# Six edits to a two-layer decoder trunk: where the step sizes' projection stands, the order within a weight block, column tiles, row tiles, held blocks and the last norm

## The chip, the cores and the metric

The kernel runs on one core of one Trainium2 chip. The metric is the device time of one execution in microseconds (us). Three runs of the kernel before took 1283.12, 1284.42 and 1284.76; the median is 1284.42.

The names in the profile: PE is TensorE's matmuls, PEld its weight loads, DVE is VectorE, ACT is ScalarE, POOL is GpSimd, and SPq and POOLq are the queues on which SyncE and GpSimd issue DMAs.

## The reference

A residual stream `x` of 256 tokens by 2048 passes through two layers, each followed by `x = layer_norm(alpha * x + mixer(x))`, all in float32. Cut to what matters here:

```python
# layer 0: Mamba-2 SSD, 64 heads of 64 channels in 8 groups, state 128
z, xbc, dt = split(x @ w_in)                 # 4096 | 6144 | 64
xs, bm, cm = split(silu(conv4(xbc)))         # 4096 | 1024 | 1024
dt = softplus(dt + dt_bias)                  # the step sizes, 64 per token
y  = (cb * decay) @ (xs * dt) + d_skip * xs  # cb = cm @ bm.T, per head, causal
yg = rms_norm_per_group(y * silu(z)) * norm_g
h  = yg @ w_out                              # 4096 -> 2048
# layer 1: sparse attention, 32 heads of 128, latent of 256
c_q, c_kv, k_idx, w_idx, gate = split(x @ w_in)
s     = relu(q_idx @ k_idx.T)                # 16 index heads of 64
score = sum_over_heads(s * w_idx)            # causal; the best 64 keys stay
o     = softmax(masked(q_lat @ c_kv.T)) @ c_kv
h     = (uv(o) * silu(gate)) @ w_out         # 4096 -> 2048
```

## The kernel before

**Exact products from halves.** Weights arrive as blocks of 128 x 1024 (512 KB). ACT copies each to a rounded `hi` (L97) and DVE subtracts to get `lo` (L98). Activations are kept the same way, as a high and a low part side by side (`xT`, `yg`, `x1T`, `og`). A float32 product is then three rounded ones: hi by hi, hi by lo, lo by hi. Small products (`y`, `cb`, `ms`, `p_dt`, the scores, the attention) run in plain float32, which the profile shows as two matmuls for each one in the program.

**The stream.** The class `Stream` sets the order. Its units are the weight blocks in program order: 160 for layer 0's input projection, 64 for its output, 16 for layer 1's latents (three pairs of gate blocks behind them), 4 for the index queries, 32 for the heads mixed with the other gates (32 gates, two blocks each), and 64 for the last output projection. `run` first converts up to four blocks ahead (`SPLIT`), then issues a unit's matmuls, then one step of each active generator. `side(i, ...)` starts such a generator at unit `i`, so all small work is strewn between the units' matmuls in steps. `load` runs four blocks ahead of the conversion (`RAW`), on SPq. Both `hi` and `lo` have four buffers.

**A block of a column projection** (`stream_w`, with `mm3`): eight k-tiles of 128. For each a 512-wide matmul of `hi` with both parts of the activations, and then a 256-wide one of `lo` with the high part (L260, L261), into one PSUM tile `acc` (`g` for the gates).

**The start.** x comes in four quarters of 512 KB, with the weight blocks between them and `w_dt` behind. Units 0 and 1 run, then the 16 products of `p_dt` (L573), then the rest. `dt_steps` makes the step sizes from `p_dt`.

**A group of layer 0** is 20 units: B, C, four tiles of x, four of z. `m_steps` makes the decay products `M`, two heads to a step, `xst_steps` transposes x (`pxs`), and `y_steps(g, c)` multiplies them for one pair of heads: four products whose stationary side is 64 columns wide, written to PSUM partitions 0 to 63 or 64 to 127 (L391). DVE adds the skip and multiplies by the gate, ACT squares, and POOL adds the squares up over the four tiles. At the group's end a product with `sel` (1/512 in one column, 64 wide) sums them over the channels (`ms`, L412), and `norm_steps` runs for every second group.

**The scores** (`idx_steps`, L745 and L747): the keys of 64 channels lie twice in `kp`, once in the upper and once in the lower rows, with zeros in the other half, so that one product over 128 rows gives two index heads.

**The end** (`out_proj` and `last`): the last output projection makes four column blocks of 512 for two halves of 128 tokens. For the last one, the half-1 products of the last four weight blocks are held back, and follow the half-0 products, first their left 256 columns, then the right ones into the tile `part`. After that come the residual, the statistics, the inverse root in small steps (`rsqrt1_steps`), two steps over each of four 512-wide pieces (centre and gain; scale and offset), and the stores. The steps over some pieces run on ACT and POOL (`center_p`, `scale_p`), the others on DVE.

Of the kernel before, what the change touches and what calls it, by code (L numbers as in the profile page):

```python
# [16 lines left out]
P = 128  # L17
T = 256
# [34 lines left out]
HELD = 6  # L53
AHEAD = 2
# [69 lines left out]
def trunk_kernel(ctx: ExitStack, tc: tile.TileContext, x, xt, w1, wdt, dtp, prm, wo1,  # L124
# [46 lines left out]
    sel = cpool.tile([P, 2, 64], F32, tag="sel", name="sel")  # L171
# [85 lines left out]
    def mm3(ps, hk, lk, both, first, last):  # L257


        nc.tensor.matmul(ps, hk, both, start=first, stop=False, skip_group_check=True)  # L260
        nc.tensor.matmul(ps[:, 0:T], lk, both[:, 0:T], start=False, stop=last,  # L261
                         skip_group_check=True)
# [120 lines left out]
    def y_steps(g, c):  # L383
        ms = G[g].pop(("M", c))
        py = y_tile(f"y{g}_{c}")
        xsT = G[g][("xsT", c // 2)]
        for s in (0, 1):
            ws = slice(s * 256, 256 + s * 128)
            for k in (0, 1):
                ks = slice(64 * k, 64 * k + 64)  # L390
                nc.tensor.matmul(py[ks, s * P:T], xsT[:, s, c % 2, ks], ms[k][:, ws],  # L391
                                 start=(s == 0), stop=(s == 1), skip_group_check=True)
        yield
        vt = G[g][("x", c)]
        j = PC_SKIP + g * 4 + c
        v.scalar_tensor_tensor(vt, vt, par[:, j:j + 1], py[:, 0:T], op0=ALU.mult, op1=ALU.add)
        v.tensor_mul(vt, vt, G[g].pop(("z", c)))
        yield
        sq = sp2.tile([P, T], F32, tag="sq", name=f"sq{g}_{c}", bufs=3)
        nc.scalar.activation(sq, vt, AF.Square)  # L400
        yield
        if c:
            nc.gpsimd.tensor_add(sq, sq, G[g].pop("sq"))
        G[g]["sq"] = sq
        if c < 3:
            return
# [5 lines left out]
        nc.tensor.matmul(MS[b][0:64, 0:T], sel[:, k, :], sq, start=(k == 0), stop=(k == 1))  # L412
        yield
# [120 lines left out]
    for g in range(NG):  # L534
# [30 lines left out]
    split_x(0, 4)  # L565
    st.convert_to(1)
    split_x(4, 8)
    split_x(8, 12)
    st.convert_to(2)
    split_x(12, 16)  # L570
    st.run(DT_AT)
    for kt in range(KT):
        nc.tensor.matmul(p_dt[0:NH1, 0:T], w_dt[:, kt, :], xr[:, kt, :],  # L573
                         start=(kt == 0), stop=(kt == KT - 1))
    v.tensor_scalar_mul(convh, par[:, PC_CONV:PC_CONV + 240], 0.5)
# [113 lines left out]
    def kidx_steps(cell):  # L689
# [43 lines left out]
    def idx_steps(q, cell):  # L733
# [7 lines left out]
        for k in range(2):  # L741
            c = 2 * q + k
            pa = y_tile(f"sa{c}")
            pb = m_tile(f"sb{c}")
            nc.tensor.matmul(pa, qx[:, k, P:T], kp.rearrange("p a b -> p (a b)"),  # L745
                             start=True, stop=True)
            nc.tensor.matmul(pb[:, 0:T], qx[:, k, 0:P], kp[:, :, 0:P], start=True, stop=True)  # L747
# [453 lines left out]
```

## Time and profile before

| what | value |
|---|---|
| median of 3 runs | 1284.42 us |
| the profiled execution: its own time, its span | 1286.14 us, 1284.3 us |
| granted TensorE clock, mean | 0.991 |
| costliest on PE: `acc` L260, L261 | 458.3 us x1280, 360.3 us x1280 |
| `y` L391 on PE, 256 and 128 wide | 20.9 us x128, 12.4 us x128 |
| scores on PE: `sa` L745, `sb` L747 | 8.2 us x16, 4.8 us x16 |
| `ms` L412, `p_dt` L573 on PE | 5.2 us x16, 7.1 us x32 |
| splits: `hi` L97 on ACT, `lo` L98 on DVE | 423.7 us x404, 489.9 us x404 |
| first matmul, end of the last one | 7.23 us, 1265.87 us |

A row of the timeline has the start (us from the span's start), the duration, the engine, the line, the operation, out<-in with the shape, a count where equal rows are merged, and in brackets the idle time before it and what ended that. A row of a group has a count, then busy us and the mean ns of one, then idle time. A row of the waits has the sum, how many, the longest. Rows of PE overlap, since matmuls are pipelined; the end of one is modelled.

### The profile page before, as it was taken

The page shows a single profiled execution, that of the slowest core. Times are in us where ns is not written, and L with a number is a line of the kernel's source. Part 1 is how long each engine was busy: PE and PEld are TensorE (multiplying, and loading weights), DVE is VectorE, ACT ScalarE, POOL GpSimd, SP SyncE. Part 2 cuts the span into 40 slices and gives each one's busy share as a digit, 9 for nine tenths or more (in the row PEclk, how much of TensorE's full clock was granted, in tenths as well). Part 3 has the DMA queues.
Part 4 walks back from the last instruction along what each step waited for, and adds up shares of the span by engine and source line. Part 5 has one row for each costly group of instructions (what it writes and reads, how often), then busy time and mean ns, then how long its engine had stood idle before and what let it go on. Part 6 is the DMA issues. An engine that isn't in the chain of part 4 may idle for free.

```text
span 1284.3 us, 19045 instructions
## 1 busy us (share of the span) xinstructions
PE 1251.2 (97%) x7034; PEld 1069.6 (83%) x7034; DVE 915.9 (71%) x1680; ACT 702.0 (55%) x1194; POOL 83.8 (7%) x113
## 2 busy tenths in 40 slices
PE   7999999999999999999998999999999999999994
PEld 5888888888888888788886797999999998888883
DVE  5978787988798879756457577856666656566456
ACT  4556565656566666444335455566566666433332
POOL 1001111101110111110000000000000001000003
PEclk9999999999999999999999999999999999999997
DMA  7665566665656666676664463554444445866651
GB/s 254 207 193 181 181 182 194 178 205 175 204 176 195 182 198 179 179 249 203 197 191 156 164 220 129 181 164 148 158 155 149 148 154 166 336 208 189 195 179 66
DMA packets 65148, 236.51 MB, mean 184 GB/s; under 512 B 7896, under 2 KB 7904, under 8 KB 64672
## 3 DMA queue, kind: packets, MB, share of 16 engines
q1 hardware_dynamic: 60048, 215.12, 52.7%
q0 software_dynamic: 5008, 20.19, 4.6%
q8 instruction: 55, 0.90, 0.3%
q14 instruction: 37, 0.30, 0.1%
HBM read 231.00 MB, written 4.28 MB: 183 GB/s over the span
## 4 chain that ended last, share of the span: by engine, by line
PE 94%; DVE 3%; DMA 1%; ACT 1%; issue 0%; SPq 0%; DVEq 0%
PE acc L260 24%; PE acc L261 12%; PE g L260 9%; PE o L485 9%; PE o L486 8%; PE o L487 8%; PE g L261 5%; PE y L391 2%; PE q L814 1%; PE q L816 1%; PE q L815 1%; PE lg L832 1%; PE o L863 1%; PE pt L856 1%; PE pxs L373 1%; DMA scr<-in_xt_dram 1%
## 5 line engine op out<-in xcount | busy, mean ns | idle before, releaser
L98 DVE TENSOR_TENSOR lo<-raw,hi 128x1024 fp32r<-128x1024 f32 (+1 forms) x404 | 489.9, 1215 | 295.3 <-ACT hi L97 294.2
L97 ACT ACTIVATE hi<-raw 128x1024 fp32r<-128x1024 f32 (+1 forms) x404 | 423.7, 1051 | 314.9 <-PE o L487 171.8
L260 PE MATMUL acc<-xT,hi 128*128 128x512 f32 x1280 | 458.3, 402 | 8.1 <-DVE xT L553 8.1
L261 PE MATMUL acc<-xT,lo 128*128 128x256 f32 x1280 | 360.3, 282 | 0.4 <-DVE lo L98 0.4
L260 PEld LDWEIGHTS acc<-xT,hi 128*128 128x128 f32 x1280 | 241.6, 189 | 69.3 <-ACT hi L97 7.4
L261 PEld LDWEIGHTS acc<-xT,lo 128*128 128x128 f32 x1280 | 243.2, 190 | 0.9 <-DVE lo L98 0.9
L260 PE MATMUL g<-x1T,hi 128*128 128x512 f32 x512 | 188.2, 408 | 0.0
L261 PE MATMUL g<-x1T,lo 128*128 128x256 f32 x512 | 143.4, 280 | 0.0
L260 PEld LDWEIGHTS g<-x1T,hi 128*128 128x128 f32 x512 | 96.1, 188 | 21.2
L485 PE MATMUL o<-hi,yg 128*128 128x512 f32 x256 | 100.4, 392 | 0.0
L486 PE MATMUL o<-lo,yg 128*128 128x512 f32 x256 | 99.7, 390 | 0.0
L487 PE MATMUL o<-hi,yg 128*128 128x512 f32 x256 | 99.7, 389 | 0.0
L485 PE MATMUL o<-hi,og 128*128 128x512 f32 (+1 forms) x256 | 99.5, 389 | 0.0
L487 PE MATMUL o<-hi,og 128*128 128x512 f32 (+1 forms) x256 | 98.9, 386 | 0.0
L486 PE MATMUL o<-lo,og 128*128 128x512 f32 (+1 forms) x256 | 98.8, 386 | 0.0
L261 PEld LDWEIGHTS g<-x1T,lo 128*128 128x128 f32 x512 | 96.8, 189 | 0.5
L295 DVE SCALAR_TENSOR_TENSOR ca<-cr,convh,ca 128x255 f32<-128x255 f32 x144 | 69.3, 481 | 3.4
L485 PEld LDWEIGHTS o<-hi,yg 128*128 128x128 f32 x256 | 48.1, 188 | 10.9 <-issue 0.7
L487 PEld LDWEIGHTS o<-hi,yg 128*128 128x128 f32 x256 | 48.0, 188 | 10.1
L487 PEld LDWEIGHTS o<-hi,og 128*128 128x128 f32 x256 | 48.1, 188 | 9.9
L486 PEld LDWEIGHTS o<-lo,yg 128*128 128x128 f32 x256 | 48.1, 188 | 9.8
L485 PEld LDWEIGHTS o<-hi,og 128*128 128x128 f32 x256 | 48.1, 188 | 9.6
(246 smaller groups left out, 1688.5 us busy)
## 6 DMA issues: line engine op xcount, KB each, us to landing
raw<-in_w_dram SPq DMA_DIRECT2D x160, 512.0 KB, 3.9
raw<-in_wo_dram SPq DMA_DIRECT2D x128, 512.0 KB, 4.3
raw<-in_wg_dram SPq DMA_DIRECT2D x64, 512.0 KB, 3.3
raw<-in_wab_dram SPq DMA_DIRECT2D x32, 512.0 KB, 3.2
abc<-acs_d POOLq DMA_DIRECT2D x32, 256.0 KB, 4.1
raw<-in_wcq_dram SPq DMA_DIRECT2D x8, 512.0 KB, 4.4
raw<-in_wkv_dram SPq DMA_DIRECT2D x8, 336.0 KB, 6.3
scr<-in_xt_dram SPq DMA_DIRECT2D x4, 512.0 KB, 8.1
```

The source lines that it names most:

```text
L97: self.nc.scalar.activation(h[:, :w], r[:, :w], AF.Copy)
L98: eng.tensor_sub(l[:, :w], r[:, :w], h[:, :w].bitcast(F32))
L260: nc.tensor.matmul(ps, hk, both, start=first, stop=False, skip_group_check=True)
L261: nc.tensor.matmul(ps[:, 0:T], lk, both[:, 0:T], start=False, stop=last, skip_group_check=True)
L295: v.scalar_tensor_tensor(acc[:, d:], rw[:, :T - d], w(k), acc[:, d:], op0=ALU.mult, op1=ALU.add)
L373: nc.tensor.transpose(pm[:, o:o + P], G[g][("x", 2 * half + c)][:, s * P:(s + 1) * P], ident)
L391: nc.tensor.matmul(py[ks, s * P:T], xsT[:, s, c % 2, ks], ms[k][:, ws], start=(s == 0), stop=(s == 1), skip_group_check=True)
L485: nc.tensor.matmul(ps, ah, hs, start=(kk == 2 * first), stop=False)
L486: nc.tensor.matmul(ps, ah, ls, start=False, stop=False)
L487: nc.tensor.matmul(ps, al, hs, start=False, stop=(kk == 31))
L814: nc.tensor.matmul(ps, h[:, o:o + P], cqT[:, kt, 0:T], start=(kt == 0), stop=False)
L815: nc.tensor.matmul(ps, h[:, o:o + P], cqT[:, kt, T:2 * T], start=False, stop=False)
```

## The change

What it does, in six parts:
1. `w_dt` is the first transfer, x comes before the first weight block, and `p_dt`'s products stand before all units.
2. In `stream_w` the eight matmuls with `hi` come first, then the eight with `lo`; `mm3` is gone.
3. `y_steps` takes two pairs of heads at once, into two halves of one PSUM tile; it starts with the second pair's step. `sel` is 128 wide. The sum `ms` and the norm come one unit later.
4. The scores: `kp` holds the keys once in each half of the rows, without zeros. One index head's queries and keys lie in rows 0 to 63 and go to the tile `sa`, the other's in rows 64 to 127 and go to `sb`. ACT takes each tile in one 384-wide step.
5. Eight blocks are held at the end (`LAST`): the first four run 512 wide, the last four as before. The last four blocks get buffers of their own, in the room of the heads' pool, which is closed 24 units before the end.
6. The last norm runs on DVE alone. Each piece is stored after its scaling.

```diff
+LAST = 8
...
-    sel = cpool.tile([P, 2, 64], F32, tag="sel", name="sel")
+    sel = cpool.tile([P, 2, P], F32, tag="sel", name="sel")
...
             for k in range(8):
-                kt, ks = half * 8 + k, slice(k * P, (k + 1) * P)
-                mm3(cell["ps"], h[:, ks], l[:, ks], cell["x"][0][:, kt, :], kt == 0, kt == 15)
+                kt = half * 8 + k
+                nc.tensor.matmul(ps, h[:, k * P:(k + 1) * P], xs[:, kt, :], start=(kt == 0),
+                                 stop=False, skip_group_check=True)
+            for k in range(8):
+                kt = half * 8 + k
+                nc.tensor.matmul(ps[:, 0:T], l[:, k * P:(k + 1) * P], xs[:, kt, 0:T],
+                                 start=False, stop=(kt == 15), skip_group_check=True)
...
-    def y_steps(g, c):
-        ms = G[g].pop(("M", c))
+    def y_steps(g, half):
+        py = y_tile(f"y{g}_{half}")
+        xsT = G[g][("xsT", half)]
+        ms = [G[g].pop(("M", 2 * half + c)) for c in (0, 1)]
+        for c in (0, 1):
+            for s in (0, 1):
+                ws = slice(s * 256, 256 + s * 128)
+                for k in (0, 1):
+                    ks = slice(64 * k, 64 * k + 64)
+                    nc.tensor.matmul(py[ks, c * T + s * P:(c + 1) * T], xsT[:, s, c, ks],
+                                     ms[c][k][:, ws], start=(c == 0 and s == 0),
+                                     stop=(s == 1), skip_group_check=True)
...
-        nc.tensor.matmul(MS[b][0:64, 0:T], sel[:, k, :], sq, start=(k == 0), stop=(k == 1))
+        nc.tensor.matmul(MS[b][:, 0:T], sel[:, k, :], sq, start=(k == 0), stop=(k == 1))
...
-            st.side(u + 18 + max(gap * c, 2 * c), (y_steps, g, c))
+            if c % 2:
+                st.side(u + 18 + max(gap * c, 2 * c), (y_steps, g, c // 2))
...
-    load_x(0, 4)
-    st.load(0)
+    nc.sync.dma_start(w_dt, wdt)
+    load_x(0, 2)
+    load_x(2, 4)
     load_x(4, 8)
     load_x(8, 12)
-    st.load(1)
+    st.load(0)
     load_x(12, 16)
-    st.load(2)
-    nc.sync.dma_start(w_dt, wdt)
-    for i in range(3, RAW):
+    for i in range(1, RAW):
         st.load(i)
...
-            nc.tensor.matmul(pa, qx[:, k, P:T], kp.rearrange("p a b -> p (a b)"),
-                             start=True, stop=True)
-            nc.tensor.matmul(pb[:, 0:T], qx[:, k, 0:P], kp[:, :, 0:P], start=True, stop=True)
+            for a, w, b, n in ((P, T, 0, T), (0, P, T, P)):
+                for j in range(2):
+                    js = slice(64 * j, 64 * j + 64)
+                    nc.tensor.matmul(pj[j][:, b:b + n], qx[js, k, a:w], kp[js, 0:n],
+                                     start=True, stop=True, skip_group_check=True)
...
+        def normed2(half):
+            mv, rs, steps = mean(half)
+            for n in range(4):
+                next(steps, None)
+                next(steps, None)
+                center(half, n, mv)
+            now(steps)
+            for n in range(4):
+                scale(half, n, rs)
...
-        for a in held:
+        k = len(held) - 4
+        for a in held[:k]:
+            mm(*a, 1)
+        for a in held[k:]:
             mm(*a, 1, cols=(0, 256))
...
+    st.run(n_heads + 40)
+    heads.close()
+    wmore = ctx.enter_context(tc.tile_pool(name="wlast", bufs=4))
+    for i in range(len(st.units) - 4, len(st.units)):
+        st.homes[i] = wmore
```

Three places in the order of instructions. The first is PE at the end of group 1 of layer 0 and the beginning of group 2, before: the sum `ms`, the transposes `pxs` and the first `y` of group 2.

```order
L412 MATMUL ms_1398<-sq_3_1311,sel 64x256
L373 MATMUL pxs_1_1403<-ident,xs_2_1275 128x128 x2
L373 MATMUL pxs_1_1403<-ident,xs_3_1344 128x128 x2
L391 MATMUL y_0_1408<-M_1313,xsT_0_1240 64x256
L391 MATMUL y_0_1408<-M_1315,xsT_0_1240 64x256
L391 MATMUL y_0_1408<-M_1313,xsT_0_1240 64x128
L391 MATMUL y_0_1408<-M_1315,xsT_0_1240 64x128
L260 MATMUL acc_1381<-xT,hi_1321 128x512
```

The same place of the change, on PE: the transposes, one unit, the sum.

```order
L375 MATMUL pxs_1_1400<-ident,xs_2_1269 128x128 x2
L375 MATMUL pxs_1_1400<-ident,xs_3_1342 128x128 x2
L267 MATMUL acc_1380<-xT,hi_1319 128x512 x8
L271 MATMUL acc_1380<-xT,lo_1320 128x256 x8
L424 MATMUL ms_1433<-sq_3_1308,sel 128x256
```

And, four units further on, its first `y` of two pairs of heads.

```order
L395 MATMUL y_0_1551<-M_1311,xsT_0_1234 64x256
L395 MATMUL y_0_1551<-M_1313,xsT_0_1234 64x256
L395 MATMUL y_0_1551<-M_1311,xsT_0_1234 64x128
L395 MATMUL y_0_1551<-M_1313,xsT_0_1234 64x128
L395 MATMUL y_0_1551<-M_1466,xsT_0_1234 64x256
L395 MATMUL y_0_1551<-M_1468,xsT_0_1234 64x256
L395 MATMUL y_0_1551<-M_1466,xsT_0_1234 64x128
L395 MATMUL y_0_1551<-M_1468,xsT_0_1234 64x128
```

Before, `ms` and `y` stood with `pxs` in one stretch; now each of the three stands by itself, `ms` one unit later and `y` five, with twice the products.

The second place is the head of SP's queue, before (`scr` holds x and `w_dt`, `raw` the weight blocks):

```order
L549 DMA scr<-in_xt_dram 128x1024
L86 DMA raw_121<-in_w_dram 128x1024
L549 DMA scr<-in_xt_dram 128x1024 x2
L86 DMA raw_125<-in_w_dram 128x1024
L549 DMA scr<-in_xt_dram 128x1024
L86 DMA raw_128<-in_w_dram 128x1024
L562 DMA scr<-in_wdt_dram 128x1024
L86 DMA raw_131<-in_w_dram 128x1024
```

And SP's queue in the change:

```order
L568 DMA scr<-in_wdt_dram 128x1024
L562 DMA scr<-in_xt_dram 128x512 x2
L562 DMA scr<-in_xt_dram 128x1024 x2
L87 DMA raw_125<-in_w_dram 128x1024
L562 DMA scr<-in_xt_dram 128x1024
L87 DMA raw_128<-in_w_dram 128x1024
```

`w_dt` has moved from the eighth place to the first, and the first weight block from the second to behind three quarters of x.

The third place is DVE's last stretch, before: half 1 from its statistics (`t` and `rs` are the inverse root's steps, L1049 centres, L1053 scales).

```order
L1038 BN_AGGR mv_12509<-st_6175 128x2
L1039 TENSOR_SCALAR nm_12510<-mv_12509 128x1
L1040 TENSOR_SCALAR ve_12512<-mv_12509 128x1
L190 TENSOR_SCALAR t_12513<-ve_12512 128x1
L1049 SCALAR_TENSOR_TENSOR fin<-fin,mv_12509 128x512
L192 TENSOR_SCALAR rs_12511<-t_12513 128x1
L1049 SCALAR_TENSOR_TENSOR fin<-fin,mv_12509 128x512
L195 TENSOR_SCALAR t_12513<-rs_12511,ve_12512 128x1
L1053 SCALAR_TENSOR_TENSOR fin<-fin,rs_12480 128x512
L197 SCALAR_TENSOR_TENSOR rs_12511<-t_12513,rs_12511 128x1
L1053 SCALAR_TENSOR_TENSOR fin<-fin,rs_12480 128x512
```

And DVE's in the change, from the same step on:

```order
L1046 BN_AGGR mv_12511<-st_6160 128x2
L1047 TENSOR_SCALAR ve_12513<-mv_12511 128x1
L191 TENSOR_SCALAR t_12514<-ve_12513 128x1
L193 TENSOR_SCALAR rs_12512<-t_12514 128x1
L1056 SCALAR_TENSOR_TENSOR fin<-fin,mv_12511 128x512
L196 TENSOR_SCALAR t_12514<-rs_12512,ve_12513 128x1
L198 SCALAR_TENSOR_TENSOR rs_12512<-t_12514,rs_12512 128x1
L1056 SCALAR_TENSOR_TENSOR fin<-fin,mv_12511 128x512
```

Before, half 0's last scalings (with `rs_12480`) stood between half 1's steps, and some of half 1's centrings were on ACT and POOL; now all four of each half are DVE's, and half 0's stand ahead of half 1's.

More of the change, by code (lines that the diff above doesn't have):

```diff
@@ L255, in dt_steps @@
         yield
[L257 to L262, printed above, removed]
     def stream_w(half, cell, name):
@@ L381, in xst_steps @@
         yield
-    def y_steps(g, c):
-        ms = G[g].pop(("M", c))
[L385 to L392, printed above, removed]
-        yield
[L394 to L397, printed above, removed]
+    def y_steps(g, half):
[10 more added lines that the diff above has]
+                                     stop=(s == 1), skip_group_check=True)
+        yield
+        vts = [G[g][("x", 2 * half + c)] for c in (0, 1)]
+        for c, vt in enumerate(vts):
+            j = PC_SKIP + g * 4 + 2 * half + c
+            v.scalar_tensor_tensor(vt, vt, par[:, j:j + 1], py[:, c * T:(c + 1) * T],
+                                   op0=ALU.mult, op1=ALU.add)
+            v.tensor_mul(vt, vt, G[g].pop(("z", 2 * half + c)))
         yield
-        sq = sp2.tile([P, T], F32, tag="sq", name=f"sq{g}_{c}", bufs=3)
-        nc.scalar.activation(sq, vt, AF.Square)
+        sqs = [sp2.tile([P, T], F32, tag="sq", name=f"sq{g}_{2 * half + c}", bufs=3)
+               for c in (0, 1)]
+        for vt, sq in zip(vts, sqs):
+            nc.scalar.activation(sq, vt, AF.Square)
         yield
-        if c:
+        if half == 0:
+            nc.gpsimd.tensor_add(sqs[1], sqs[1], sqs[0])
+            G[g]["sq"] = sqs[1]
+            return
+        for sq in sqs:
             nc.gpsimd.tensor_add(sq, sq, G[g].pop("sq"))
-        G[g]["sq"] = sq
-        if c < 3:
-            return
+            G[g]["sq"] = sq
+        yield
         yield
@@ L700, in kidx_steps @@
         yield
-        for k in range(2):
-            ks = slice(64 * k, 64 * k + 64)
-            v.tensor_copy(A["kp"][ks, k, :], pm[ks, 0:T])
+        v.tensor_copy(A["kp"], pm[:, 0:T])
         yield
@@ L1071, in last @@
+        for a in held[k:]:
             mm(*a, 1, cols=(0, 256))
-        for a in held:
-            mm(*a, 1, part=part[:, 0:256], cols=(256, 512), first=held[0][1])
+        for a in held[k:]:
+            mm(*a, 1, part=part[:, 0:256], cols=(256, 512), first=held[k][1])
         c3 = r[:, 1, 1536:2048]
         now(residual2(3, 0, cell))
-        mv, nm, rs, steps = mean(0)
-        for n in (0, 1, 3):
-            center_p(0, n, nm)
-        next(steps)
-        center(0, 2, mv)
-        for _ in range(3):
-            next(steps)
+        normed2(0)
@@ L1084, in last @@
         v.scalar_tensor_tensor(c3, c3, ALPHA, cell["ps"][1], op0=ALU.mult, op1=ALU.add)
-        next(steps)
         v.bn_stats(sts[:, 1, 6, :], c3[:, 0:256])
-        now(steps)
-        scale_p(0, 0, rs)
-        scale_p(0, 1, rs)
-        rs0 = rs
         v.tensor_add(c3[:, 256:512], c3[:, 256:512], part[:, 0:256])
         v.bn_stats(sts[:, 1, 7, :], c3[:, 256:512])
-        mv, nm, rs, steps = mean(1)
-        center_p(1, 0, nm)
-        center_p(1, 1, nm)
-        for n in (2, 3):
-            next(steps)
-            center(1, n, mv)
@@ L1099, in last @@
-        for n in (2, 3):
-            next(steps)
-            scale(0, n, rs0)
-        for n in (0, 1, 2, 3):
-            store(0, n)
-        now(steps)
-        scale_p(1, 0, rs)
-        for n in (2, 1, 3):
-            scale(1, n, rs)
-        for n in (2, 1, 0, 3):
-            store(1, n)
+        normed2(1)
     L["tail2"] = last
```

61 lines of the change are left out of this document (24 added, 37 removed).

## The prediction

> **What bounds the kernel now.** I read the page from its top, then TensorE's waits, then the timeline of single places: a run of the stream, the start, a switch, the end.
>
> ```profile
> PE 1251.2 (97%) x7034; PEld 1069.6 (83%) x7034; DVE 915.9 (71%) x1680; ACT 702.0 (55%) x1194; POOL 83.8 (7%) x113
> PE 94%; DVE 3%; DMA 1%; ACT 1%; issue 0%; SPq 0%; DVEq 0%
> PE acc L260 <- DVE xT L553: 8.1, 2, 7.2
> ```
>
> TensorE is busy 97% of the span and is 94% of the chain that ended last; its largest wait is the 8.1 us at the start. So between the first and the last matmul nearly nothing but fewer or shorter steps on TensorE saves time. Matmuls overlap, so a row's duration is not its price: the price is the distance from its start to the next start, and I use such distances. The rest of the time lies at the two ends, before TensorE starts and after its last matmul.
>
> **First all high parts of a block, then all low ones.** Rows: first and last of 21 pairs in a row, of 11 pairs, of 66 matmuls 512 wide, of six such, and of 23 that are 256 wide; then the weight loads and the split on DVE.
>
> ```profile
> 112.94 0.40 PE L260 MATMUL acc<-xT,hi 128*128 128x512 f32 x1
> 120.36 0.40 PE L260 MATMUL acc<-xT,hi 128*128 128x512 f32 x1
> 123.85 0.39 PE L260 MATMUL acc<-xT,hi 128*128 128x512 f32 x1
> 127.66 0.39 PE L260 MATMUL acc<-xT,hi 128*128 128x512 f32 x1
> 1240.23 0.39 PE L485 MATMUL o<-hi,og 128*128 128x512 f32 x1
> 1255.19 0.39 PE L485 MATMUL o<-hi,og 128*128 128x512 f32 x1
> 698.27 0.39 PE L612 MATMUL qp<-hi,x1T 128*128 128x512 f32 x1
> 699.66 0.39 PE L612 MATMUL qp<-hi,x1T 128*128 128x512 f32 x1
> 1262.83 0.28 PE L485 MATMUL part<-hi,og 128*128 128x256 f32 x1
> 1265.59 0.28 PE L487 MATMUL part<-hi,og 128*128 128x256 f32 x1
> L261 PEld LDWEIGHTS acc<-xT,lo 128*128 128x128 f32 x1280 | 243.2, 190 | 0.9 <-DVE lo L98 0.9
> L98 DVE TENSOR_TENSOR lo<-raw,hi 128x1024 fp32r<-128x1024 f32 (+1 forms) x404 | 489.9, 1215 | 295.3 <-ACT hi L97 294.2
> ```
>
> A pair costs 0.353 in the long run (7.42 / 21) and 0.346 in the other (3.81 / 11); between them 0.351, nearer to the longer. Alone, 512-wide matmuls cost 0.227 (`o`) or 0.232 (`qp`), 256-wide ones 0.120. A block of eight pairs is 2.81 us now; grouped it would be 8 x 0.227 + 8 x 0.120 = 2.78, or 2.82 with 0.232. There are 224 such blocks (160 and 64). The ends are -11 us (0.227 throughout, and 0.117 for the low ones) and +2; I take **-5.0 us**, from 0.227, which the longer of the two rows has, and low ones between 0.117 and 0.120. That the low parts are needed later saves nothing: TensorE hardly waits for them (0.9 us in the row of the loads).
>
> The Trainium skill ("TensorE: Matmul & The Clock Gate", Part 3, The mechanism, on what overlaps and what doesn't) says that a weight load overlaps matmuls in flight only when its row group differs. By that rule the eight low matmuls would each pay their load; the trace disagrees so far, with 0.120 between starts.
>
> **The step sizes' projection first.** ACT's first rows start when a transfer of 512 KB has landed: the first, the fifth and the sixth of the queue. Then come a 512-wide matmul of that time, and `p_dt` with what follows it.
>
> ```profile
> 4.76 1.06 ACT L552 ACTIVATE xT<-scr 128x1024 fp32r<-128x1024 f32 x1 [2.68 <-DMA scr<-in_xt_dram]
> 11.99 1.06 ACT L97 ACTIVATE hi<-raw 128x1024 fp32r<-128x1024 f32 x1 [0.23 <-DMA raw<-in_w_dram]
> 13.47 1.06 ACT L552 ACTIVATE xT<-scr 128x1024 fp32r<-128x1024 f32 x1 [0.41 <-DMA scr<-in_xt_dram]
> 12.60 0.63 PE L260 MATMUL acc<-xT,hi 128*128 128x512 f32 x1
> 17.82 7.12 PE L573 MATMUL p_dt<-scr 128*64 128x256 f32 x32
> 24.87 0.50 PE L260 MATMUL acc<-xT,hi 128*128 128x512 f32 x1
> ```
>
> The 16 products of `p_dt` take 7.05 us, 0.44 each, where TensorE has other work. In the changed queue `w_dt` is first, x's quarters are transfers 2, 3, 4 and 6 (the first of them cut in two), and the first weight block is transfer 5. So `p_dt` can start at about 5.4 (4.76 and half a transfer), and its last four products wait for transfer 6: they end at 13.47 + 4 x 0.44 = 15.2 at the earliest. But TensorE is slow at first: 0.63 us at 12.60 where the runs above have 0.39. With products at double price until about 13 us they end near 16.2. Block 0 landed at 11.99 and is split by 14.3; its 8 pairs and the next 8 take 5.6. The third block starts at 21.8, not 24.87: **-3.1 us**. Bounds: -4.1 (end at 15.2) and +0.8 (double price for all 16, about 14 us from 5.4 and a gap, an end at 20).
>
> **Heads' outputs by four, ones 128 wide.** The first four rows show one `y` between two pairs, the next two the sum of squares `ms`. Then come the scores, which use the whole array.
>
> ```profile
> 104.81 0.28 PE L261 MATMUL acc<-xT,lo 128*128 128x256 f32 x1
> 105.02 0.87 PE L391 MATMUL y<-M,xsT 128*64 128x256 f32 x8
> 105.82 0.50 PE L260 MATMUL acc<-xT,hi 128*128 128x512 f32 x1
> 106.15 0.28 PE L261 MATMUL acc<-xT,lo 128*128 128x256 f32 x1
> 136.07 0.65 PE L412 MATMUL ms<-sq,sel 128*64 128x256 f32 x2
> 136.65 0.66 PE L373 MATMUL pxs<-ident,xs 128*128 128x128 f32 x4
> ...
> 771.57 0.28 PE L730 MATMUL ix<-cqT,lo 128*128 128x256 f32 x1
> 771.69 1.02 PE L745 MATMUL sa<-sC 128*128 128x512 f32 x2
> 772.55 0.59 PE L747 MATMUL sb<-sC 128*128 128x256 f32 x2
> 772.80 0.47 PE L728 MATMUL ix<-cqT,hi 128*128 128x256 f32 x1
> 773.11 0.28 PE L729 MATMUL ix<-cqT,hi 128*128 128x256 f32 x1
> ```
>
> A 512-wide float32 product costs 0.86 us (`sa` to `sb`), 1.68 ns a column. From 771.57 to 773.11 are 1.54 us: 1.29 of products and 0.24 of the two 256-wide matmuls beside them. Entry and exit cost 0.01 while the whole array is used. In `y`, two products on 64 columns run side by side, so its 384 columns should take 0.65. From 104.81 to 106.15 are 1.34, less 0.35 for one pair: 0.99. Switching to half the columns and back costs **0.34 us**. `ms` is 64 wide too and shows the exit: 0.58 for 256 columns, not 0.43. There are 32 switches for `y` and 8 for `ms`; 16 stay. 24 x 0.34 = **-8.2 us**. Bounds: -5.4 if `ms` gains nothing, and -8.6. The steps of DVE, ACT and POOL for `y` stay the same in number and lie beside TensorE's stream.
>
> One wait is new: in the last group the third `M` needs a buffer that the first `y` of four still reads, so DVE stands until that `y` is done. Behind it stand one more `M`, one `xsT`, two `E` and the next `lo`, none longer than `lo`'s 1.2 us; I estimate 4. TensorE has two blocks split ahead, 24 matmuls of 0.227, 5.4 us: 0, at worst 1.
>
> **Scores on row halves.** Eight times 1.29 now, half of it products with zeros. If the halves run side by side as `y`'s do, they take 8 x 0.65 = 5.2, and the five places where they stand switch to half the rows: 5 x 0.34 = 1.7. So 10.3 becomes 6.9: **-3.4 us**. No row shows two row halves. Bounds: -5.1 (the switch is free) and +1.7 (one after the other). I take side by side, from `y`, the nearest row. The Trainium skill ("TensorE: Matmul & The Clock Gate", Part 3, The mechanism) says that tiles on different row groups overlap; no run here shows it.
>
> **The end.** DVE's rows, then the stores.
>
> ```profile
> 1262.39 0.74 DVE L1049 SCALAR_TENSOR_TENSOR fin<-fin,mv 128x512 f32<-128x512 f32 x1
> 1266.78 0.41 DVE L1091 TENSOR_TENSOR fin<-fin,part 128x256 f32<-128x256 f32 x1
> 1268.34 0.15 DVE L190 TENSOR_SCALAR t<-ve 128x1 int32<-128x1 int32 x1
> 1269.56 1.68 DVE L1049 SCALAR_TENSOR_TENSOR fin<-fin,mv 128x512 f32<-128x512 f32 x1
> 1274.63 0.26 DVE L195 TENSOR_SCALAR t<-rs,ve 128x1 f32<-128x1 f32 x1
> 1275.12 0.27 DVE L195 TENSOR_SCALAR t<-rs,ve 128x1 f32<-128x1 f32 x1
> 1275.62 3.08 DVE L1053 SCALAR_TENSOR_TENSOR fin<-fin,rs 128x512 f32<-128x512 f32 x3
> out_dram<-fin SPq DMA_DIRECT2D x8, 256.0 KB, 2.0
> ```
>
> TensorE ends at 1265.59 + 0.28 = 1265.9, DVE at 1278.7: 12.8 us. DVE is late because half 0 is not finished when TensorE is, and because the same step that takes 0.74 takes 1.68 beside POOL's work. With eight blocks held, half 1 takes 24 x 0.227 + 48 x 0.120 = 11.2 us behind half 0, and half 0's chain (statistics, then the steps below, some 9 us) ends before that. After TensorE's end remain: the sum and the statistics, 1.6 (1266.78 to 1268.34); eight steps at about 0.70, 5.6; the inverse root, three rounds of 0.49, in part hidden between them, and its start, 1.4. Together 8.6: **-4.2 us**. The last store lands 2.0 us behind 1278.7, and the span ends 3.5 us after that, at 1284.3, with no row there. POOL has no work left at the end, which may shorten this by 0 to 3: I take **-1.5**. Term: **-5.7**, bounds -3 and -7.5. For this, the held blocks must be split at one per six matmuls, 1.36 us; DVE's 1.2 fits, with little to spare.
>
> **Sum.** -5.0 - 3.1 - 8.2 - 3.4 - 5.7 = **-25.4 us**. The profiled execution took 1286.1 (its span and 1.8 around it), 1.7 over the median of 1284.4. So 1260.7 for such an execution, and 1259.0 as a median.
>
> **Rivals.**
> - The row halves run one after the other (against: `y`; for: no row): five us less gain, 1284.4 - 20.3 = 1264.1.
> - The grouped stream gains nothing or loses up to 2 (for: `qp` at 0.232): 1264 to 1266.
> - Start and end give nothing, because the slow clock stretches `p_dt` and DVE meets another wait: 1267.8.
> - Slower: the eight low loads in a row are not hidden. If the low matmuls came at the load's 0.190 instead of 0.117, that is 1792 x 0.073 = +131, and with the other four terms (-20.4) 1395. It decides from 11 ns per low matmul, 0.128 between starts. Against it: 0.120 in 23 gaps, each with a load of its own. The rule quoted above would give this.
>
> **Chances.** Forecast 0.60; row halves 0.13; grouping 0.16; start and end 0.05; exposed loads 0.04; nothing of it shows 0.02. Within 0.2% a measurement of this kernel can't tell a difference from none. Faster 0.94, same 0.02, slower 0.04. The range takes the good ends of grouping and tail together below, and lost row halves with lost grouping above: 1249 to 1272.
>
> **What would show it.** `p_dt` done before 17 us and the third block before 23; 16 `y`, each about 1.6 us between its neighbours, and `ms` as cheap as the scores' entry; `sa` and `sb` starting within 0.02 us of each other; eight 512-wide starts at 0.227 to 0.232, then eight near 0.12; DVE's last step some 8.6 us behind TensorE's last matmul. Wrong if the low starts lie at 0.13 or more, if `sa` and `sb` start 0.2 apart, or if TensorE shows new waits for `hi` or `lo`.

## The result, and the profile after

Four runs of the changed kernel took 1260.48 to 1262.22 us, median **1261.53**; before, four runs took 1283.12 to 1284.76, median 1284.41. The ratio is **0.9823, 95% interval 0.9810 to 0.9837**: faster by 1.8%, 2.5 us short of the forecast median of 1259.0 and inside the predicted range. The profiled execution took 1262.22, its span is 1260.5; before, the span was 1284.3. Two executions among the experiments took far longer (3182.70 us in u10_y_early, 2524.32 in u12_group_alone) and are in no ratio below; without them the medians of these two are 1259.99 and 1282.00.

The page of the changed kernel, its first part and the shares of the chain that ended last, and then TensorE's waits (us in total, times, longest):

```profile
PE 1235.4 (98%) x7066; PEld 1072.6 (85%) x7066; DVE 909.4 (72%) x1685; ACT 692.3 (55%) x1186; POOL 68.6 (5%) x104
PE 93%; DVE 4%; DMA 1%; issue 1%; ACT 0%; SPq 0%; DVEq 0%; ACTq 0%
```

```profile
PE p_dt L578 <- DMA scr<-in_xt_dram: 6.0, 3, 5.3
PE o L497 <- DVE zs L278: 0.8, 1, 0.8
PE cb L324 <- DVE C L306: 0.3, 1, 0.3
PE pxs L375 <- DVE xs L306: 0.3, 1, 0.3
```

TensorE is still what bounds the kernel. The wait at the start is 2 us shorter, and three small waits are new, all for VectorE; the largest is that of the first output projection for `zs`.

Where the time went can be read stretch by stretch. The table is worked out from the starts of the matmuls in the two traces. "Blocks" is the sum of the distances from one matmul of the stream to the next; "small work" is the sum of the distances from a block's last matmul to the next block's first, where anything stands between them (what it delays behind that first matmul counts as blocks). The prediction's -5.0 for grouping is spread over the 224 blocks.

| stretch (us) | before | after | measured | predicted |
|---|---|---|---|---|
| to the third block | 24.87 | 20.82 | -4.05 | -3.1 |
| third block to first `qp`: blocks | 443.4 | 440.7 | -2.7 | -3.5 |
| the same stretch: small work (`y`, `ms`, `pxs`, `cb`) | 47.7 | 40.4 | -7.35 | -8.2 |
| the same stretch: the first output projection | 180.1 | 180.6 | +0.5 | 0 |
| first `qp` to the first head (with the scores) | 116.8 | 113.3 | -3.6 | -3.8 |
| heads, gates, last output projection | 452.8 | 452.9 | +0.1 | -1.1 |
| last matmul's end to the span's end | 18.4 | 11.7 | -6.7 | -5.7 |
| sum | | | -23.8 | -25.4 |

The rows of the changed kernel's timeline that answer to those shown before: the start; one `y` of four heads between two blocks; one `ms`; the first scores.

```profile
5.32 3.62 PE L578 MATMUL p_dt<-scr 128*64 128x256 f32 x8 [5.32 <-DMA scr<-in_xt_dram]
9.41 3.67 PE L578 MATMUL p_dt<-scr 128*64 128x256 f32 x16 [0.47 <-DMA scr<-in_xt_dram]
13.25 1.94 PE L578 MATMUL p_dt<-scr 128*64 128x256 f32 x8 [0.17 <-DMA scr<-in_xt_dram]
15.12 2.11 PE L267 MATMUL acc<-xT,hi 128*128 128x512 f32 x8
...
20.82 2.00 PE L267 MATMUL acc<-xT,hi 128*128 128x512 f32 x8
...
83.78 1.11 PE L271 MATMUL acc<-xT,lo 128*128 128x256 f32 x8
84.82 1.52 PE L395 MATMUL y<-M,xsT 128*64 128x256 f32 x16
86.27 2.14 PE L267 MATMUL acc<-xT,hi 128*128 128x512 f32 x8
...
133.27 1.11 PE L271 MATMUL acc<-xT,lo 128*128 128x256 f32 x8
134.22 0.59 PE L424 MATMUL ms<-sq,sel 128*128 128x256 f32 x2
134.46 2.20 PE L267 MATMUL acc<-xT,hi 128*128 128x512 f32 x8
...
757.96 0.48 PE L756 MATMUL sa<-sC 64*128 64x256 f32 x1
757.97 0.48 PE L756 MATMUL sb<-sC 64*128 64x256 f32 x1
758.28 0.38 PE L756 MATMUL sa<-sC 64*128 64x256 f32 x1
758.29 0.38 PE L756 MATMUL sb<-sC 64*128 64x256 f32 x1
```

The first eight matmuls of `p_dt` take 3.62 us and the next sixteen 3.67: TensorE is at half speed only for the first ones. `y` of four heads takes 1.45 (84.82 to 86.27) where two `y` before took 2 x 0.80; `ms` takes 0.24 where it took 0.58. `sa` and `sb` start 0.01 apart, and the next two 0.32 later, again together: the row halves do run side by side.

The end: TensorE's last matmul, VectorE's last steps, the stores (start of the first issue, and time to the end of the last one; the stores take 2.1 us to land).

```profile
1248.51 0.28 PE L499 MATMUL part<-hi,og 128*128 128x256 f32 x1
1248.83 0.42 DVE L1088 TENSOR_TENSOR fin<-fin,part 128x256 f32<-128x256 f32 x1 [1.20 <-PE part L499]
1254.38 2.73 DVE L1060 SCALAR_TENSOR_TENSOR fin<-fin,rs 128x512 f32<-128x512 f32 x4
1244.61 12.87 SPq L1062 DMA_DIRECT2D out_dram<-fin  x8
```

VectorE now waits for TensorE (1.20 us) before it closes half 1: half 0 was done in time. It ends at 1257.1, 8.3 us behind TensorE (12.8 before), and the span ends 3.4 us after that (5.6 before).

### The profile page after: what moved, and what is told of

Its sections match the earlier page's. It is cut to its first block, busy times and chain, and to the rows that moved or that the text cites. A ratio compares the mean times of both kernels' runs of the same rounds, so it can differ in the third digit from the quotient of the medians.

```text
span 1260.5 us, 19096 instructions
## 1 busy us (share of the span) xinstructions
PE 1235.4 (98%) x7066; PEld 1072.6 (85%) x7066; DVE 909.4 (72%) x1685; ACT 692.3 (55%) x1186; POOL 68.6 (5%) x104
## 4 chain that ended last, share of the span: by engine, by line
PE 93%; DVE 4%; DMA 1%; issue 1%; ACT 0%; SPq 0%; DVEq 0%; ACTq 0%
PE acc L267 22%; PE acc L271 11%; PE g L267 9%; PE o L497 9%; PE o L499 9%; PE o L498 9%; PE g L271 5%; PE y L395 2%; DVE lo L99 1%; PE q L822 1%; PE q L823 1%; PE q L824 1%; PE lg L840 1%; PE o L871 1%; PE pt L864 1%; DMA scr<-in_xt_dram 1%
## 5 line engine op out<-in xcount | busy, mean ns | idle before, releaser
L267 PE MATMUL acc<-xT,hi 128*128 128x512 f32 x1280 | 324.7, 395 | 0.0
L267 PEld LDWEIGHTS acc<-xT,hi 128*128 128x128 f32 x1280 | 230.3, 189 | 43.0 <-ACT E L350 0.9
L271 PEld LDWEIGHTS acc<-xT,lo 128*128 128x128 f32 x1280 | 174.5, 190 | 12.8
L271 PE MATMUL acc<-xT,lo 128*128 128x256 f32 x1280 | 178.3, 282 | 0.0
L267 PE MATMUL g<-x1T,hi 128*128 128x512 f32 x512 | 134.2, 404 | 0.0
L267 PEld LDWEIGHTS g<-x1T,hi 128*128 128x128 f32 x512 | 92.8, 188 | 17.9
L271 PEld LDWEIGHTS g<-x1T,lo 128*128 128x128 f32 x512 | 69.8, 190 | 5.1
L271 PE MATMUL g<-x1T,lo 128*128 128x256 f32 x512 | 71.3, 282 | 0.0
L300 ACT ACTIVATE cr<-ca 128x256 f32<-128x256 f32 x48 | 20.1, 418 | 88.1 <-DVE ca L297 88.1
L499 PEld LDWEIGHTS o<-hi,og 128*128 128x128 f32 x256 | 48.1, 188 | 9.9
```

Of the source, the lines that this page charges most:

```text
L267: nc.tensor.matmul(ps, h[:, k * P:(k + 1) * P], xs[:, kt, :], start=(kt == 0), stop=False, skip_group_check=True)
L271: nc.tensor.matmul(ps[:, 0:T], l[:, k * P:(k + 1) * P], xs[:, kt, 0:T], start=False, stop=(kt == 15), skip_group_check=True)
L300: nc.scalar.activation(rw, acc, AF.Tanh)
L499: nc.tensor.matmul(ps, al, hs, start=False, stop=(kk == 31))
```

## The experiments

Twelve kernels, each timed in five rounds against the kernel before, whose medians in the three series were 1283.44, 1283.49 and 1283.58. Since these differ a little from the 1284.41 beside the changed kernel, the last column compares ratios: the variant's less 0.9823, times 1284. Each ratio has an interval of about +-0.0013, 1.7 us, so a difference in that column under some 2.4 us is not sure by the times alone; there the stretches of the trace have to carry the reading. A drop of the granted clock that lasts 3.4 us in some traces and 6.8 in others makes about 1 us of difference between them (last section).

| variant | median us | ratio, 95% interval | against the changed kernel, us |
|---|---|---|---|
| u1_pairs | 1260.02 | 0.9815 (0.9802 to 0.9829) | -1.0 |
| u8_mirror | 1261.02 | 0.9824 (0.9810 to 0.9837) | +0.1 |
| u2_y_by_two | 1265.41 | 0.9862 (0.9848 to 0.9875) | +5.0 |
| u6_ones64 | 1263.91 | 0.9844 (0.9831 to 0.9858) | +2.7 |
| u3_scores_full | 1264.23 | 0.9849 (0.9836 to 0.9863) | +3.3 |
| u7_start_before | 1265.13 | 0.9857 (0.9844 to 0.9871) | +4.4 |
| u4_last4 | 1265.26 | 0.9855 (0.9842 to 0.9868) | +4.1 |
| u5_act_pool_norm | 1266.30 | 0.9863 (0.9849 to 0.9876) | +5.1 |
| u10_y_early | 1260.12 | 0.9820 (0.9806 to 0.9833) | -0.4 |
| u11_pairs_y_early | 1261.82 | 0.9830 (0.9816 to 0.9843) | +0.9 |
| u12_group_alone | 1282.12 | 0.9987 (0.9978 to 0.9996) | (before, one part) |
| u13_y_four_alone | 1274.53 | 0.9931 (0.9917 to 0.9945) | (before, one part) |

### What is the grouping of high and low parts worth?

**u1_pairs**: the changed kernel with part 2 undone, a high and a low matmul in turn.

```diff
                 nc.tensor.matmul(ps, h[:, k * P:(k + 1) * P], xs[:, kt, :], start=(kt == 0),
                                  stop=False, skip_group_check=True)
-            for k in range(8):
-                kt = half * 8 + k
                 nc.tensor.matmul(ps[:, 0:T], l[:, k * P:(k + 1) * P], xs[:, kt, 0:T],
```

> The changed kernel with part 2 alone undone: each high matmul is followed by its low one again. Theory A: grouping is worth what the clean blocks show, 2.81 us a block in pairs and 2.79 grouped, about half of that behind a burst; over 224 blocks +2.5 to +4 us, so 1264 to 1265.5, and clean blocks of 2.81 us again. Rival: the order within a block is worth nothing and the gain of the stretch is all from fewer switches: 1261.5. Rival: weight loads were what grouping changed: then 256-wide starts would differ between the two orders by more than 0.01 us.

Measured: 1260.02, not slower at all. The theory that grouping gives 2.5 to 4 us in this kernel fell. Little is left of the -1.0 either: its five executions have granted clocks of 0.995 and 0.996 and spans of 1257.1 to 1258.6, and the two of the changed kernel at 0.996 have 1258.5 and 1259.0 (its other two, at 0.994, have 1260.1 and 1260.5). **u8_mirror**, the high parts first in a tile's first block and the low parts first in its second, so that runs of equal matmuls become twice as long:

```diff
...
+            for part in ((highs, lows), (lows, highs))[half]:
+                part()
```

> The changed kernel with the two blocks of a column in mirrored order: high, low, then low, high, so that runs of one width are twice as long. Theory A (a change of width costs): in the changed kernel the first five 512-wide starts behind a low run are 0.228 to 0.236 and the later ones 0.227, about 26 ns a block; half as many changes make a block 10 to 13 ns shorter, -2 to -3 us: 1259. Rival (the uneven starts come at any place, whatever the widths): 1261.5. Rival (what made the blocks shorter is only that highs stand together): 1261.5.

Measured: 1261.02, no difference by the times. In the trace the blocks between two other blocks take 2.785 us in the mean, 0.008 less than grouped ones, but from the third block to the first `qp` only 0.6 us are gained (661.2 against 661.8), not 2 to 3. So the number of changes between high and low matmuls is at most a small part of it; the pairs, which change most often, can be faster still. The timelines show it. First the changed kernel (two blocks from row to row), then u1_pairs (20 pairs from the first row to the last):

```profile
303.11 2.00 PE L267 MATMUL acc<-xT,hi 128*128 128x512 f32 x8
...
308.69 2.00 PE L267 MATMUL acc<-xT,hi 128*128 128x512 f32 x8
```

```profile
304.76 0.39 PE L267 MATMUL acc<-xT,hi 128*128 128x512 f32 x1
...
311.69 0.39 PE L267 MATMUL acc<-xT,hi 128*128 128x512 f32 x1
```

A grouped block takes 5.58 / 2 = 2.79 us; eight pairs here take 8 x 6.93 / 20 = 2.77, less than grouped. The kernel before had pairs of 0.353 and of 0.346, and so has u1_pairs, in another mixture. I counted the blocks of the stream from 40 us on that stand between two other blocks, by the distance from their first matmul to the next block's first:

| kernel | counted | 2.77 | 2.79 | 2.82 to 2.83 | mean |
|---|---|---|---|---|---|
| before | 83 | 26 | 0 | 57 | 2.810 |
| after | 83 | 0 | 83 | 0 | 2.793 |
| u1_pairs | 83 | 63 | 0 | 20 | 2.786 |
| u11_pairs_y_early | 82 | 33 | 0 | 49 | 2.806 |
| u12_group_alone | 83 | 0 | 83 | 0 | 2.793 |
| u13_y_four_alone | 84 | 71 | 0 | 13 | 2.782 |

Pairs run in one of two phases and keep it, as a rule, until other work interrupts the blocks; grouped blocks always take the value between. That makes a new theory: what grouping gains depends on how many pairs were in the slow phase, and with `y` by four, where the change has it, most are in the fast one. Two parts alone, put on the kernel before, test it. **u12_group_alone** has `stream_w` of the changed kernel and nothing else; **u13_y_four_alone** has `y_steps` by two pairs of heads, the norm one unit later and the 128 wide `sel`, and nothing else:

```diff
-            st.side(u + 18 + max(gap * c, 2 * c), (y_steps, g, c))
+            if c % 2:
+                st.side(u + 18 + max(gap * c, 2 * c), (y_steps, g, c // 2))
```

> The kernel before with the grouping of high and low parts alone. Theory A (pairs run in one of two phases, 2.77 or 2.83 us a block, the mixture of before has 2.811 in the mean; grouped blocks have 2.793 always): some 150 blocks of the stream by 0.018, 2.5 to 3 us faster than before, about 1280.7. Theory B (the prediction, 5.0 us): 1278.5. Theory C (grouping changes nothing, as it seemed beside the other parts): 1283.5.

> The kernel before with the heads' outputs by four and the matrix of ones 128 wide alone; high and low parts stay in pairs. Theory A (the switches that go also leave the pairs more often in the fast phase): 24 switches of 0.34, 8.2 us, and some 3 to 4 us from blocks at a mean of 2.79 in place of 2.811, less 0.8 of the stall before the first output projection: 10.5 to 11.5 us faster than before, about 1272.5. Rival (only the switches): 7.4 us, about 1276, with blocks of 2.81 us as before.

Measured: 1282.12 for grouping alone, 1.5 us faster than before (interval 0.5 to 2.8); its trace has -3.1 in the blocks, as Theory A had it, and the time lies between A and C. For `y` by four alone 1274.53, 8.9 us faster (7.1 to 10.7), between A and its rival. Its trace, from the third block to the first `qp`: blocks 443.4 to 439.3, so -4.1 without any grouping; small work -6.75; output projection +1.0. The blocks' mean of 2.785 over all that were counted, gates too, is A's; its time is not, since the small work gave less than 8.2. Together with u1_pairs, whose blocks sum to 439.9 against 440.7 grouped: **grouping is worth some 3 us in the blocks of the kernel before and nothing, or about -0.8, beside `y` by four in its place in the change.** The two parts don't add there. It is the place that counts, not only the four: with `y` one block earlier (u10_y_early and u11_pairs_y_early below) grouped blocks sum to 440.4 and pairs to 442.2, so grouping is worth 1.8 again.

### What does a switch of the array cost?

**u2_y_by_two**: `y_steps` for one pair of heads again, `sel` stays 128 wide. **u6_ones64**: `sel` 64 wide again, `y` stays by four. Their edits, one after the other:

```diff
-            if c % 2:
-                st.side(u + 18 + max(gap * c, 2 * c), (y_steps, g, c // 2))
+            st.side(u + 18 + max(gap * c, 2 * c), (y_steps, g, c))
```

```diff
-    sel = cpool.tile([P, 2, P], F32, tag="sel", name="sel")
+    sel = cpool.tile([P, 2, 64], F32, tag="sel", name="sel")
```

> The changed kernel with y by two heads again (32 stretches of four products, not 16 of eight); the ones stay 128 wide, all else as changed. Theory A: a switch to 64 columns and back costs 0.34 to 0.36 us, so 16 more cost +5.6 us, and the stall of 0.9 us at the beginning of the first output projection goes, since DVE's work for y is spread again: +4.7, 1266. Rival: the switches are free and the gain of that stretch came from the order within the blocks: 1261 to 1262.

> The matrix of ones is 64 columns wide again, so that its eight matmuls put TensorE's array to half width and back; the heads' outputs stay by four. If a switch costs 0.34 us wherever it stands: 8 x 0.34 = 2.7 us slower than the changed kernel, about 1264.2. Rival (a single narrow matmul is not the same as a group of them, its cost lies in the products): about 1261.5.

Measured: +5.0 and +2.7. In the traces the small work of the stretch rises from 40.4 to 45.8 and to 43.0. The price of one switch is read from single places, by the way from the first low matmul of the block ahead to the last high one of the block behind, against 2.57 us where nothing stands between them. A `y` of two heads adds 0.99 (14 places of u2_y_by_two), one of four 1.67 (7 places of the changed kernel): 2 x 0.99 - 1.67 = 0.32 for the switch that is saved. An `ms` adds 0.78 at 64 wide (6 places of u6_ones64) and 0.44 at 128 (6 places of the changed kernel): 0.346 before rounding, 0.35. One `ms` of u6_ones64 between two blocks:

```profile
133.03 1.11 PE L271 MATMUL acc<-xT,lo 128*128 128x256 f32 x8
134.07 0.65 PE L424 MATMUL ms<-sq,sel 128*64 128x256 f32 x2
134.65 2.12 PE L267 MATMUL acc<-xT,hi 128*128 128x512 f32 x8
```

The same product takes 0.58 to the next start, not 0.24, and starts 1.04 behind the first of the eight, not 0.95; of these 0.43 us the first high matmul behind the 128 wide `ms` gives back 0.08 (0.42 to the next start, 0.34 behind the narrow one). The price is paid once per switch and is nearly the same whether one product stands behind it (`ms`) or several (`y`). The Trainium skill ("TensorEngine Tiling (Array Packing)", Key Properties) says that "Changing tiling mode (not just tile) drains the TensorE", without a price; the 0.32 and 0.35 us agree with it, and are a price.

### The scores

**u3_scores_full**: the scores as before, 128 rows with zeros in half of the keys.

```diff
-            for a, w, b, n in ((P, T, 0, T), (0, P, T, P)):
-                for j in range(2):
...
+            nc.tensor.matmul(pa, qx[:, k, P:T], kp.rearrange("p a b -> p (a b)"),
+                             start=True, stop=True)
+            nc.tensor.matmul(pb[:, 0:T], qx[:, k, 0:P], kp[:, :, 0:P], start=True, stop=True)
...
```

> The changed kernel with the scores over 128 rows again (keys twice, zeros in the other half). Theory A: the row halves run side by side and save 8 x 0.65 = 5.1, less five switches of 0.4 = 2: +3.2 us, 1264.7. Rival: the stretch's 3.4 us came from elsewhere (the gates between, DVE): 1261.5.

Measured: +3.3, and from the first index query to the first head 49.69 us where the changed kernel takes 46.55, so 3.1. The row halves are worth what was predicted.

### The start

**u7_start_before**: the queue and the place of `p_dt` as before.

```diff
-    nc.sync.dma_start(w_dt, wdt)
-    load_x(0, 2)
-    load_x(2, 4)
+    load_x(0, 4)
+    st.load(0)
...
+    st.run(DT_AT)
+    for kt in range(KT):
+        nc.tensor.matmul(p_dt[0:NH1, 0:T], w_dt[:, kt, :], xr[:, kt, :],
...
```

> The start of the program is as before: x and the first weight blocks are asked for ahead of the step sizes' weights, and the projection of the step sizes stands behind the first two blocks. All else as in the changed kernel. Theory A (the 4.05 us that the third block starts earlier are carried to the end undiminished): 1265.5. Rival (the stream that starts earlier meets a wait further on, so that part of it is given back): 1262 to 1264, with the wait seen in the stream before the first output projection.

```profile
7.16 2.05 PE L267 MATMUL acc<-xT,hi 128*128 128x512 f32 x4 [7.16 <-ACT hi L98]
...
17.11 7.12 PE L586 MATMUL p_dt<-scr 128*64 128x256 f32 x32
24.16 2.11 PE L267 MATMUL acc<-xT,hi 128*128 128x512 f32 x8
```

Measured: +4.4; the third block starts 3.34 later than in the changed kernel (24.16 against 20.82). From there to the first `qp` it takes 661.7 us, the changed kernel 661.8: nothing is given back. The start itself varies from trace to trace: the third block begins at 20.08 to 21.16 in the ten traces with the new start and at 23.87 to 24.87 in the four with the old one. The means, 20.7 and 24.3, are 3.5 us apart.

### The end

**u4_last4**: `LAST = 4`, so four blocks held, the norm on VectorE. **u5_act_pool_norm**: eight held, the norm's steps on ACT and POOL as before. The edit of the first, and of the second the part with the held blocks (`last` is otherwise that of before):

```diff
-LAST = 8
+LAST = 4
```

```diff
+        k = len(held) - 4
+        for a in held[:k]:
+            mm(*a, 1)
-        for a in held:
+        for a in held[k:]:
             mm(*a, 1, cols=(0, 256))
```

> Four blocks instead of eight are held back at the end; the last norm stays on VectorE. In the changed kernel VectorE ends its work on the first row half at 1247.6 and then waits 1.2 us for TensorE's last product; with four blocks fewer behind the first half, 24 matmuls of 0.227 us (5.4 us) are no longer there to lie over it. Theory A (the end got shorter because the first half's norm now lies beside matmuls): 5.4 less the 1.2 us of slack, 4.2 us slower than the changed kernel, about 1265.7, with VectorE done some 13 us behind TensorE's last matmul instead of 8.4. Theory B (the norm's move to VectorE alone made the end shorter, and holding blocks does nothing): about 1261.5.

> The last norm is done as before, with steps on ScalarE and GpSimd beside VectorE, but with eight blocks held. Theory A (held blocks shorten the end by about 4 of the 6.7 us measured, the norm's place by the rest): about 1264, and the span ends some 5.5 us behind VectorE's last step, as before, not 3.4. Theory B (only the norm's place counts): 1268. Theory C (only the held blocks count, the steps beside GpSimd cost nothing): 1261.5.

First u4_last4, then u5_act_pool_norm: the last matmul, VectorE's last steps, POOL's last, the stores.

```profile
1247.68 0.27 PE L499 MATMUL part<-hi,og 128*128 128x256 f32 x1
1257.71 2.73 DVE L1060 SCALAR_TENSOR_TENSOR fin<-fin,rs 128x512 f32<-128x512 f32 x4
1249.24 11.56 SPq L1062 DMA_DIRECT2D out_dram<-fin  x8
```

```profile
1247.15 0.28 PE L499 MATMUL part<-hi,og 128*128 128x256 f32 x1
1250.35 1.68 DVE L1057 SCALAR_TENSOR_TENSOR fin<-fin,mv 128x512 f32<-128x512 f32 x1
1255.35 3.08 DVE L1061 SCALAR_TENSOR_TENSOR fin<-fin,rs 128x512 f32<-128x512 f32 x3
1256.21 1.68 POOL L1071 TENSOR_TENSOR fin<-fin 128x512 f32<-128x512 f32 x1 [3.06 <-ACT fin L1070]
1248.62 10.17 SPq L1075 DMA_DIRECT2D out_dram<-fin  x8
```

| us | VectorE's end behind the last matmul | span's end behind that | sum |
|---|---|---|---|
| before: four held, ACT and POOL | 12.8 | 5.6 | 18.4 |
| u4_last4: four held, VectorE | 12.5 | 3.4 | 15.8 |
| u5_act_pool_norm: eight held, ACT and POOL | 11.0 | 5.6 | 16.6 |
| after: eight held, VectorE | 8.3 | 3.4 | 11.7 |

u4_last4 came out as Theory A said (+4.1). u5_act_pool_norm cost +5.1: more than A's 2.5 and less than B's 6.5, so neither part alone makes the end. Held blocks alone save 1.8, the norm's place alone 2.5, both 6.7: with eight held, half 0 is out of the way, and only then do VectorE's shorter steps (0.74 us in place of up to 1.68 beside POOL's work) shorten the way from TensorE's end to VectorE's. The 2.2 us at the very end go with the norm on ACT and POOL: 5.6 in both kernels that have it there, 3.4 in both that don't. They lie behind the stores, which take 2.0 to 2.1 us to land in all four. No run takes ACT and POOL apart.

### The new wait before the first output projection

The changed kernel: VectorE's steps on `y`, its step on `zs`, and the output projection that waits for it, since it needs the PSUM tile that `zs` reads.

```profile
490.50 0.47 DVE L402 SCALAR_TENSOR_TENSOR xs<-xs,par,y 128x256 f32<-128x256 f32 x1
...
491.86 0.43 DVE L404 TENSOR_TENSOR xs<-xs,zs 128x256 f32<-128x256 f32 x1
...
503.48 0.41 DVE L278 TENSOR_TENSOR zs<-acc,zs 128x256 f32<-128x256 f32 x1
504.04 0.47 PE L497 MATMUL o<-hi,yg 128*128 128x512 f32 x1 [0.77 <-DVE zs L278]
506.48 1.03 DVE L363 TENSOR_TENSOR M<-E,cbm 128x384 f32<-128x384 f32 x2 [1.46 <-PE y L395]
```

From 487.7 to 505.0 VectorE has no idle time, and the four steps on `y` (490.50 to 492.2) stand early in it. u2_y_by_two, which has two of them in one place, has no such wait. **u10_y_early** puts `y` one block earlier; **u11_pairs_y_early** does the same to u1_pairs.

```diff
-                st.side(u + 18 + max(gap * c, 2 * c), (y_steps, g, c // 2))
+                st.side(u + 17 + max(gap * c, 2 * c), (y_steps, g, c // 2))
...
-            st.side(u + 18 + gap * 3 + 7, (norm_steps, g // 2))
+            st.side(u + 18 + gap * 3 + 6, (norm_steps, g // 2))
```

> The changed kernel with the heads' outputs (and the norm behind them) one weight block earlier in the program. In the changed kernel VectorE has no idle time from 487.7 to 505 us; the four steps on y stand at 490.5 in it, and the first output projection waits 0.8 us for VectorE's zs at the end of that stretch, where it had waited 1.0 us at 486.5 for ScalarE just before. Theory A (that stall is the price of four steps in one place): one block earlier they fall into the idle 1.0 us, the wait of the output projection for zs goes, 0.8 to 1.4 us faster than the changed kernel, about 1260.5. Rival (the masks M aren't ready one block earlier, so TensorE waits for them instead): the wait for zs goes, a wait of y for M of up to 1 us in each of eight groups comes, 1262 or more.

> The same on the variant in which high and low parts alternate in pairs again (1260.0). If the two effects add: 1259.0. If the earlier place of the outputs puts the pairs back into their slow phase (blocks of 2.83 instead of 2.77 us): 1262 to 1264, with blocks of 2.83 us in the stream.

u10_y_early: the same steps, the last `zs` before the output projection, and the projection's fourth matmul.

```profile
483.74 0.47 DVE L402 SCALAR_TENSOR_TENSOR xs<-xs,par,y 128x256 f32<-128x256 f32 x1
...
500.71 0.42 DVE L278 TENSOR_TENSOR zs<-acc,zs 128x256 f32<-128x256 f32 x1
...
503.31 0.40 PE L497 MATMUL o<-hi,yg 128*128 128x512 f32 x1
```

The wait is gone, no wait for `M` came in its place, and from the third block to the first `qp` it takes 660.7 us, 1.1 less. Its median of 1260.12 is near what Theory A gave (about 1260.5), but by the ratios (-0.4) it can't be told from the changed kernel. With pairs the same edit came out at 1261.82, and the rival was right: the pairs fell back. 21 pairs of u11_pairs_y_early:

```profile
319.76 0.40 PE L267 MATMUL acc<-xT,hi 128*128 128x512 f32 x1
...
327.18 0.40 PE L267 MATMUL acc<-xT,hi 128*128 128x512 f32 x1
```

7.42 / 21 = 0.353, and its blocks sum to 442.2 us, u1_pairs' to 439.9. Moving `y` by one block thus changed what the other blocks of the stream cost. u1_pairs and u10_y_early have the lowest medians, but no variant is faster than the changed kernel by more than the intervals allow to tell.

## Why the prediction was right, and where it was off

- **Grouping (-5.0 forecast).** The term that failed. It priced pairs at the mean of before, 0.351, as if it were a property of pairs. Its own figures don't give -5.0 either: 8 x 0.351 less 8 x (0.227 + 0.120) is 0.032 a block, -7.2 over 224 blocks, and more with 0.117. Grouped blocks take 2.793, since the eight high matmuls take 1.84 (125.40 to 127.24) and not 1.82, and part 3 alone pushes pairs to 2.782. Against before the blocks gave -2.7 in the stream and nothing in the 48 gate blocks among the heads, and against pairs beside the other parts nothing (u1_pairs). The rival "gains nothing" was right of grouping beside the other parts, for a reason that it didn't name, and not of grouping against before; its time of 1264 to 1266 was not met.
- **Exposed loads (the slower rival).** Didn't occur. Eight low matmuls take 0.95 us (133.27 to 134.22), 0.119 each, under the 0.128 from which it would have decided, with a weight load of 0.190 for each. The rule of the Trainium skill quoted in the prediction ("TensorE: Matmul & The Clock Gate", Part 3, The mechanism), that loads overlap only across row groups, doesn't hold in this trace.
- **Switches (-8.2).** The price was right (0.34 forecast; 0.32 and 0.35 measured). At these prices 16 and 8 switches give 5.1 + 2.8 = 7.9; the stretch, which holds all but one of each, shows 7.35. Two new waits lie in it, of `pxs` and `cb` for VectorE, which the waits of the changed kernel list at 0.3 each.
- **"The steps for `y` lie beside TensorE's stream."** Right in number, wrong in place: four in a row delayed `zs` and made the 0.8 us wait. The wait that was forecast, VectorE standing for a free `M`, did come (1.46 at 506.48) and cost TensorE nothing, as forecast.
- **Scores (-3.4).** Right in mechanism and size; the rival of serial halves fell (starts 0.01 apart).
- **Start (-3.1, measured -4.05 in these two traces, -3.5 in the mean of all).** Mechanism right; mis-sized by the slow clock, which was taken to last until 13 us. The rows show double price until about 9.4, so `p_dt` made way at 15.12, near the forecast's own bound of 15.2.
- **End (-5.7, measured -6.7).** Mechanism right: 8.3 us behind TensorE where 8.6 was forecast, and 2.2 at the very end where 1.5 was taken.

The total is 1.6 us short of the forecast by the spans and 2.5 by the medians: grouping, switches and the new wait gave about 3.5 less than they should, start and end 2 more. That they cancel in part is luck, since they have nothing to do with each other.

## What to carry to other kernels

Price a part of a change by what the rest of the change makes of its surroundings: here two edits claimed the same 3 us, and only each alone and both together showed it. When small work is gathered into fewer and larger steps, look at the engine that takes the results as well: the same number of steps in one place can delay the release of a buffer several blocks later. A tail that two conditions hold up gives little when one of them is lifted (1.8 and 2.5 us here) and more than the sum when both are (6.7), so try them in a square of four kernels.

## What the runs showed of the hardware that was not expected

- Alternating 512 and 256 wide matmuls have two steady paces, 0.346 and 0.353 us a pair; grouped, there is one (2.793 us a block). What stood before the blocks goes with the phase, and moving other work by one block shifts many of them; what in it decides is open.
- The span ends 5.6 us behind VectorE's last step where ACT and POOL took part in the last norm, 3.4 us where POOL had not worked for long. No row shows what runs there, and which of the two engines it goes with is open.
- Between TensorE's start and its end the granted clock drops to a half once in each of the 14 traces, at the 4.2 us wait of `qp` for `lo`: for 6.8 us in the changed kernel (0.50 from 691.46 to 698.28, then 1.00), for 3.4 in u3_scores_full (0.50 from 693.60 to 696.98). While it lasts, 512-wide matmuls start 0.43 us apart, else 0.23. From the first `qp` to the first `kvp` the changed kernel therefore takes 32.47 us and u3_scores_full 31.44, with the same instructions. The seven traces with 6.8 us take 31.95 to 32.63 there, the seven with 3.4 take 31.27 to 31.48. In the long ones the drop begins 0.9 to 2.3 us before TensorE resumes, in the short ones 0.4 us before to 1.1 after. The changed kernel's four executions have mean granted clocks of 0.994 (two) and 0.996 (two), so one kernel probably has both lengths. So 1.0 us of a difference between two profiled spans may be no more than this.
